# Streaming-encoder trunk in one kernel: raw weight chunks in three slots of their own, another plan of parked and summed pairs

## The chip, the cores and the metric

One core of a Trainium2 chip runs the whole program in one launch. The metric is the device time of one execution in microseconds, the median over the runs. Profiled executions are read beside it; their span is the time from the first to the last instruction that the profiler saw.

## What is computed

Two layers over 256 positions of width 2048, all in float32. Layer 0 mixes tokens with a gated MLP with a spatial gate (gMLP), layer 1 with latent attention (MLA); both are followed by a gated MLP with a causal convolution of width 3, and each sublayer is added to its input and normalised:

```
def reference(x, ...):
    for i in range(DEPTH):                      # DEPTH = 2
        if i % N_MIXERS == 0: m = gmlp_mixer(x, ...)   # gelu(x @ w_in), layer_norm(v), gate, @ w_out
        else:                 m = mla_mixer(x, ...)    # low-rank q and kv, rotary keys, softmax, @ w_out
        x = layer_norm(ALPHA * x + m, ln_mix_g[i], ln_mix_b[i])
        f = conv_ffn(x, ...)                    # x @ w_up, convolution, silu(g) * a, @ w_down
        x = layer_norm(ALPHA * x + f, ln_ffn_g[i], ln_ffn_b[i])
    return x
```

The weights are w_in 2048 x 12288, gMLP's w_out 6144 x 2048, the MLA matrices, and for each layer w_up 2048 x 11008 and w_down 5504 x 2048.

## The kernel before

**Precision.** TensorE multiplies a reduced form of float32 (fp32r). Each float32 operand is split into a high part (a cast on ScalarE) and a low part (operand minus high part, a subtraction on VectorE), and a product takes three matmuls: high x high, low x high, high x low. All weights pass through this once: a chunk of 1 MB (128 x 2048 float32) is loaded as `raw`, ScalarE writes `wh`, VectorE writes `wl`.

**Stages.** In order: v (half of the gMLP input product, six groups of 1024 columns), u (the other half), wo (gMLP output), up0 and dn0 (the MLP of layer 0), the MLA part (mq, mkv, qr, qn, kn, vv, attention, mo), up1 and dn1. Each has a list of weight chunks; the lists are one sequence of 444 chunks, numbered from 0.

**Feed.** The class `Feed` runs through this sequence. `_load` issues a chunk's transfer on SyncE's queue (line 92 or 97), `_split` issues its cast and subtraction (lines 119, 120), and `next` keeps about two chunks split and two more loaded ahead of the chunk in use. `behind` ties each load to the last matmul issued before it in the program, so that the scheduler doesn't pull it far ahead. All these tiles (raw, wh, wl, and the activations) take slots of one pool, tag `big`, 17 slots of 8 KB per partition; a new tile takes the slot that was free first and waits for its last reader.

**Seven products.** In v, wo and dn the rows of the weight come in pairs of chunks of 128. A pair of two 128-row blocks by two 512-column blocks needs eight block products; a Winograd-like form needs seven, if four sums of the weight blocks (and of the activations) are made first. Such a pair is "seven" (`_seven`, lines 127 to 134: tile `ts` for the sums, cast and subtraction of `wh`, `wl`, `th`, `tl`), the others are "wide". Seven products spare 3 matmuls of 128 x 512 in each pair and cost VectorE and ScalarE the sums and their split. The seven sums are put together in the end by `rest` and added to the residual by `fold` (lines 431 to 434, 634).

**Parked.** For dn some pairs with seven products are split long before, during the up projection, where VectorE has time (`park`): the four results (tiles pwh, pwl, pth, ptl) are written to DRAM (`kept...`) and fetched back on GpSimd's queue (`_fetch`, line 185, tiles fwh, fwl, fth, ftl). These tiles have tag `side`, six slots.

**The plan.** `PLAN` lists for each half of the output columns the order of the pairs and the kind of each: `8s` is pair 8 with seven products, `8p` the same and parked, `8e` wide. A down projection has 22 units per half; before, 18 of 44 have seven products, 8 of these parked. `KEEP` says how many chunks ahead the activations of a kind (dn...wx, sx, px) are kept from the first half for the second.

**The end of a down projection.** The last three chunks (`SKEW`) are kept, and their products go to the accumulators one after the other, q3, p2, e and q4, so that LayerNorm (`piece`, `start`, `scale`, lines 640 to 659) can begin on the first while TensorE still works on the last. In dn1 the result then goes out to DRAM (line 659).

**What sets the order.** The program's instructions are put in order for each engine by a list scheduler, which works from the dependencies, the slots and a cost model; only what is wrapped in `keep_in_program_order` stays where it is written. So a change of slots moves instructions in many places. Within an engine the order is then fixed: an instruction that waits holds up all behind it. SyncE's order of transfers is fixed in the same way.

Of the kernel before, what the change touches and what calls it, by code (L numbers as in the profile page):

```python
# [15 lines left out]
P = 128  # L16
# [35 lines left out]
T1, T2 = 6, 5  # L52
SLOTS = {"big": 17, "side": 6}

# [17 lines left out]
class Feed:  # L72
# [73 lines left out]
    def park(self, i):  # L146
# [3 lines left out]
        add = lambda o, a, b: pin(nc.vector.tensor_tensor(o, a, b, ALU.add))  # L150
        two = lambda a, o: a[:, o : o + 1024].rearrange("p (n c) -> p n c", n=2)
        self.kept[i] = kept = {}
# [11 lines left out]
        yield  # L164
        t = tile("pts", F32)
        add(two(t, 0), two(raw, 512), raw[:, None, 0:512].to_broadcast([P, 2, 512]))
        add(t[:, 1024:1536], t[:, 0:512], raw[:, 1024:1536])
        add(t[:, 1536:2048], t[:, 1024:1536], raw[:, 1536:2048])
        yield
        for n, src, o, cols in (("w", raw, 512, 1536), ("t", t, 0, 2048)):  # L170
            hi, lo = tile(f"p{n}h", F32R), tile(f"p{n}l", F32R)
            pin(nc.scalar.copy(hi[:, 0:cols], src[:, o : o + cols]))
            pin(nc.vector.tensor_tensor(lo[:, 0:cols], src[:, o : o + cols], hi[:, 0:cols].bitcast(F32), ALU.subtract))
# [5 lines left out]
    def _fetch(self, i):  # L179

        got = []
        for n in ("wh", "wl", "th", "tl"):
            d = self.kept[i].pop(n)
            t = self.pool.tile([P, 2048], F32R, tag="side", name=f"f{n}{i}", bufs=SLOTS["side"])
            self.behind(self.nc.gpsimd.dma_start(t[:, 0 : d.shape[1]], d))
            got.append(t)
        return got

# [8 lines left out]
    def next(self, splits=2, loads=2):  # L197
        i = self.used
        self.ahead(i + 1 + splits + loads, i + 1 + splits)
        self.used += 1  # L200
        return self.parts.pop(i)


@with_exitstack
def trunk(ctx: ExitStack, tc: tile.TileContext, x, xT, gm_in, gm_wout, ffn_up, ffn_dn,
# [86 lines left out]
    for j in range(4):  # L292
        t = slot([P, 4, S], f"xraw{j}")

# [102 lines left out]
    class Banks:  # L397
# [16 lines left out]

        def seven(self, a, sums, wh, wl, th, tl):
            s1, s2, s3, s4 = sums
# [55 lines left out]
    def down(n_k, src, tag, ln, acts, skew=SKEW):  # L472
# [5 lines left out]
        for hf, units in enumerate(seq):  # L478
# [3 lines left out]
            for i, (u, kind) in enumerate(units):  # L482
# [13 lines left out]
                else:  # L496
                    acc.seven(a, sums, *got)
                    if u == last:
# [196 lines left out]
    for gi in range(6):  # L695
# [3 lines left out]
        for c, p in enumerate(V_PAIRS[gi]):  # L699
# [12 lines left out]
            if c == 2 and gi > 0:  # L712
                stats(gi - 1)
        vt = slot([P, 2, 1024], f"v{gi}", tag="side")
        for i, (n, t) in enumerate(zip(DIRECT, rest)):
# [6 lines left out]
        if gi == 0:  # L722
# [4 lines left out]
            nc.sync.dma_start(lnrow, ln_rows.rearrange("r (k p) -> (r k) p", p=P))  # L727
        if gi == 4:

            wT = slot([P, 2, 1024], "wT")  # L730
            wTg = wT[:, 0, :].rearrange("p (g i) -> p g i", g=NG)
            nc.sync.dma_start(wTg, w_sT)
            nc.gpsimd.memset(wTg[64:P, :, 0:64], 0.0)
            bsum = slot([P, 2, 1024], "bsum")
            nc.sync.dma_start(bsum[:, 1, :], b_s.to_broadcast([P, 1024]))
    stats(5)
    lnt = bank("lnrowT")
    nc.tensor.transpose(lnt[:, 0:P], lnrow, ident)
    nc.scalar.copy(lncol, lnt[:, 0:P])
    ones = tp.tile([P, P], F32, tag="t1", name="ones", bufs=T1)  # L740
    nc.gpsimd.memset(ones, 1.0)
    for f in range(2):
        rb = bank(f"rows{f}")
        mm(rb, ones, wT[:, 0, f * 512 : (f + 1) * 512], True, True)
        nc.scalar.copy(bsum[:, 0, f * 512 : (f + 1) * 512], rb)
    mv = [st.tile([P, 4], F32, tag="vmv", name=f"vmv{b}", bufs=2) for b in range(2)]
# [14 lines left out]
    rowsum = bsum[:, 0, :].rearrange("p (g i) -> p g i", g=NG)  # L761
    bsb = bsum[:, 1, :].rearrange("p (g i) -> p g i", g=NG)

# [489 lines left out]
```

## Time and profile before

| | us |
|---|---|
| median of the runs shown | 2502.89 |
| all three runs | 2502.18, 2502.89, 2507.27 |
| the profiled execution's own time | 2503.74 |
| its span | 2501.9 |
| TensorE, VectorE, ScalarE busy | 2472.1, 1987.7, 1425.2 |

The profiled execution is one more run of the same kernel; 1.84 us of its time lie outside of its span. Where a stage's length is given, it runs from one boundary that a view was asked for to the next. In the rows of a timeline the first number is the start, the second how long it took, and in brackets stands how long the engine was idle before and for what it waited. In the rows of windows, the window's bounds are followed by its length, then by each engine's busy time with its number of instructions (TensorE's matmuls, its weight loads, VectorE, ScalarE, GpSimd), the granted clock, the DMA engines' busy share, and GB/s.

### The profile page before, as it was taken

Reading aid. Unit: us, or ns where it says so; the run is one execution under the profiler, and the core shown is the slowest. Engines: PE = TensorE matmul, PEld = TensorE weight load, DVE = VectorE, ACT = ScalarE, POOL = GpSimd, SP = SyncE. Lnnn points to the kernel's source line nnn. Section 1 sums busy time; section 2 is a strip of 40 time slices with the busy share of each in tenths; the row PEclk is TensorE's granted clock in tenths of the full one; section 3 lists DMA queues with packets and bytes.
Section 4 is the critical chain, followed back from the end, with each engine's and each line's share of the span. In section 5 each row is a group of like instructions: output and inputs, shape, how many; then the busy total and the mean of one; then the engine's idle time right before and its main releaser. Section 6 shows DMA issues by size and latency. Waiting matters only on the chain.

```text
span 2501.9 us, 33396 instructions
## 1 busy us (share of the span) xinstructions
PE 2472.1 (99%) x12995; PEld 2123.2 (85%) x12995; DVE 1987.7 (79%) x2779; ACT 1425.2 (57%) x1976; POOL 84.8 (3%) x165
## 2 busy tenths in 40 slices
PE   9999999999999999999999999999999999999998
PEld 7887888888888888888887878988888888887886
DVE  6999866679898798796678878856698787768887
ACT  5666644456565666565555456564566665555543
POOL 0000000000000010000000100000000000000010
PEclk9999999999999999999999999999999999999999
DMA  6555644556566689787547984543589789556795
GB/s 245 201 217 203 218 170 169 185 178 216 201 201 214 247 337 356 293 331 277 185 168 286 341 323 165 181 168 129 189 315 352 277 340 361 200 173 231 278 375 196
DMA packets 109503, 606.17 MB, mean 242 GB/s; under 512 B 10272, under 2 KB 11040, under 8 KB 62112
## 3 DMA queue, kind: packets, MB, share of 16 engines
q1 hardware_dynamic: 85984, 465.61, 52.0%
q0 software_dynamic: 23360, 138.42, 14.1%
q8 instruction: 102, 1.67, 0.2%
q14 instruction: 57, 0.47, 0.1%
HBM read 538.98 MB, written 65.01 MB: 241 GB/s over the span
## 4 chain that ended last, share of the span: by engine, by line
PE 87%; DVE 5%; DMA 4%; issue 2%; ACT 1%; SPq 0%; POOL 0%; DVEq 0%; ACTq 0%; POOLq 0%
PE up L225 35%; PE u L225 11%; PE wo_q L225 5%; PE v_q L225 4%; PE dn_q L225 4%; PE mo L225 4%; PE v_p L225 4%; PE wo_p L225 3%; PE dn_p L225 3%; DMA raw<-in_ffn_dn_dram 3%; PE wo_e L225 2%; PE upf L225 2%; PE v_e L225 1%; DVE wl L120 1%; PE dn_e L225 1%
## 5 line engine op out<-in xcount | busy, mean ns | idle before, releaser
L120 DVE TENSOR_TENSOR wl<-raw,wh 128x1024 fp32r<-128x1024 f32 (+3 forms) x640 | 877.9, 1392 | 241.4 <-ACT wh L119 211.4
L119 ACT CAST wh<-raw 128x1024 fp32r<-128x1024 f32 (+3 forms) x640 | 743.4, 1189 | 336.2 <-DVE wl L120 71.2
L225 PE MATMUL up<-xhl,wh 128*128 128x512 f32 x2624 | 611.1, 390 | 0.0
L225 PEld LDWEIGHTS up<-xhl,wh 128*128 128x128 f32 x2624 | 487.4, 188 | 97.7
L225 PEld LDWEIGHTS up<-xhl,wl 128*128 128x128 f32 x2624 | 325.8, 192 | 6.4
L225 PE MATMUL up<-xhl,wl 128*128 128x256 f32 x2624 | 328.1, 283 | 0.0
L225 PE MATMUL u<-xhl,wh 128*128 128x512 f32 x768 | 182.5, 392 | 0.2 <-DVE h_u L380 0.2
L225 PEld LDWEIGHTS u<-xhl,wh 128*128 128x128 f32 x768 | 141.7, 188 | 29.0 <-DVE h_u L380 0.7
L127 ACT CAST th<-ts 128x1536 fp32r<-128x1536 f32 x106 | 111.2, 1052 | 86.4 <-DVE ts L134 76.0
L128 DVE TENSOR_TENSOR tl<-ts,th 128x1536 fp32r<-128x1536 f32 x106 | 126.4, 1219 | 0.6 <-ACT th L127 0.2
L225 PEld LDWEIGHTS u<-xhl,wl 128*128 128x128 f32 x768 | 95.6, 191 | 3.1 <-DVE wl L120 1.0
L127 ACT CAST wh<-raw 128x1536 fp32r<-128x1536 f32 x53 | 78.5, 1481 | 33.6 <-DVE wl L120 8.3
L225 PE MATMUL u<-xhl,wl 128*128 128x256 f32 x768 | 96.6, 283 | 0.8 <-DVE wl L120 0.8
L128 DVE TENSOR_TENSOR wl<-raw,wh 128x1536 fp32r<-128x1536 f32 x53 | 92.9, 1752 | 0.5 <-PE wo_p L225 0.4
L225 PE MATMUL mo<-wh,oT 128*128 128x512 f32 x256 | 82.6, 403 | 0.0
L134 DVE TENSOR_TENSOR ts<-raw 128x1024 f32<-128x1024 f32 x53 | 64.7, 1220 | 17.4 <-DMA raw<-in_ffn_dn_dram 10.4
L225 PE MATMUL v_q<-wh,xhl 128*128 128x512 f32 x224 | 70.2, 395 | 4.6 <-ACT wh L119 4.6
L134 DVE TENSOR_TENSOR ts<-ts,raw 128x512 f32<-128x512 f32 x106 | 72.7, 686 | 0.8
L225 PE MATMUL v_p<-wh,xhl 128*128 128x512 f32 x192 | 61.0, 395 | 1.0 <-ACT wh L119 1.0
L225 PEld LDWEIGHTS v_q<-wh,xhl 128*128 128x128 f32 x224 | 42.4, 190 | 14.4 <-ACT wh L119 5.7
L378 ACT COPY lo_u<-u 128x256 f32<-128x256 f32 x48 | 17.4, 362 | 60.0 <-PE u L225 60.0
L225 PEld LDWEIGHTS mo<-wh,oT 128*128 128x128 f32 x256 | 45.4, 189 | 7.1
(1703 smaller groups left out, 4255.2 us busy)
## 6 DMA issues: line engine op xcount, KB each, us to landing
raw<-in_ffn_up_dram SPq DMA_DIRECT2D x172, 1024.0 KB, 6.6
raw<-in_gm_in_dram SPq DMA_DIRECT2D x93, 1024.0 KB, 4.7
raw<-in_ffn_dn_dram SPq DMA_DIRECT2D x68, 1024.0 KB, 7.9
raw<-in_gm_wout_dram SPq DMA_DIRECT2D x48, 1024.0 KB, 5.1
praw<-in_ffn_dn_dram POOLq DMA_DIRECT2D x16, 1024.0 KB, 15.3
keptth<-pth POOLq DMA_DIRECT2D x16, 1024.0 KB, 9.4
kepttl<-ptl POOLq DMA_DIRECT2D x16, 1024.0 KB, 11.6
fth<-keptth POOLq DMA_DIRECT2D x16, 1024.0 KB, 9.2
```

The costliest lines, as they stand in the source:

```text
L119: self.nc.scalar.copy(hi[:, c], raw[:, c])
L120: self.nc.vector.tensor_tensor(lo[:, c], raw[:, c], hi[:, c].bitcast(F32), ALU.subtract)
L127: self.nc.scalar.copy(hi, raw)
L128: self.nc.vector.tensor_tensor(lo, raw, hi.bitcast(F32), ALU.subtract)
L134: add = lambda o, a, b: self.nc.vector.tensor_tensor(o, a, b, ALU.add)
L225: recent[0] = nc.tensor.matmul(o, l, r, start=start, stop=stop, skip_group_check=True)
L378: nc.scalar.copy(lo, acc[:, S : 2 * S])
```

## The change

**Slots.** The pool's 17 shared slots become 14, and three slots of a tag `raw` are added, which take the raw chunks only. The four pieces of the input `xraw` move from `big` to `side`. Two of the gMLP tables (`bsum` and `wT`) share fewer slots and are loaded a group later.

**Plan.** The plan of the down projection changes: parked pairs at 1, 6, 11, 15 in the first half and 19, 15, 11, 7 in the second, and nine with seven products that are not parked; 17 in all instead of 18.

**Fetch.** A parked pair is fetched when it lies within five chunks of the one in use (`LEAD`), and not when the loader comes to it.

**Park.** The sums of a parked pair are made in place, in the raw tile, by four adds of 512 columns, after the raw blocks themselves were split; the sums lie in another order, so `seven` has an offset `turned`.

**Pace.** `behind` ties no load to a matmul until the first chunk is in use.

```diff
-SLOTS = {"big": 17, "side": 6}
+SLOTS = {"big": 14, "raw": 3, "side": 6}
...
-        NF_FF: ("0e 1e 2s 3e 4p 5s 6e 7e 8s 9e 10e 11p 12s 13e 14e 15s 16e 17s 18p 19e 20e 21e",
-                "21e 20p 19e 18p 17s 16e 15p 14s 13e 12e 11p 10s 9e 8e 7p 6s 5e 4e 3e 2e 1e 0e")}
+        NF_FF: ("0e 1p 2e 3s 4e 5e 6p 7e 8s 9e 10e 11p 12e 13s 14e 15p 16e 17s 18e 19s 20e 21e",
+                "21e 20e 19p 18e 17s 16e 15p 14e 13s 12e 11p 10e 9s 8e 7p 6e 5s 4e 3e 2e 1e 0e")}
...
-KEEP = {"wide": 5, "seven": 9, "parked": 6}
+LEAD = 5
+KEEP = {"wide": 4, "seven": 6, "parked": 6}
...
         if kind == "parked":
-            self.parts[self.loaded] = self._fetch(self.loaded)
+            self.fetch(self.loaded)
             self.loaded += 1
             return
-        t = self.pool.tile([P, 2048], F32, tag="big", name=f"raw{self.loaded}", bufs=SLOTS["big"])
+        t = self.pool.tile([P, 2048], F32, tag="raw", name=f"raw{self.loaded}", bufs=SLOTS["raw"])
...
-        t = tile("pts", F32)
-        add(two(t, 0), two(raw, 512), raw[:, None, 0:512].to_broadcast([P, 2, 512]))
-        add(t[:, 1024:1536], t[:, 0:512], raw[:, 1024:1536])
-        add(t[:, 1536:2048], t[:, 1024:1536], raw[:, 1536:2048])
-        yield
-        for n, src, o, cols in (("w", raw, 512, 1536), ("t", t, 0, 2048)):
+        for n, o, cols in (("w", 512, 1536), ("t", 0, 2048)):
...
             if n == "w":
                 yield
+                r = [raw[:, 512 * i : 512 * (i + 1)] for i in range(4)]
+                add(r[1], r[1], r[0])
+                add(r[0], r[0], r[2])
+                add(r[2], r[2], r[1])
+                add(r[3], r[3], r[2])
+                yield
...
-        return self.parts.pop(i)
+        got = self.parts.pop(i)
+        near = [j for j in range(i + 1, min(i + 1 + LEAD, len(self.chunks))) if self.chunks[j][2] == "parked"]
+        if near and near[0] in self.kept:
+            self.fetch(near[0])
+        return got
...
-        if recent[0] is not None:
+        if recent[0] is not None and feed.used > 0:
...
-        t = slot([P, 4, S], f"xraw{j}")
+        t = slot([P, 4, S], f"xraw{j}", tag="side")
...
-            self.to("q5", s1, th, tl, 0)
-            self.to("p7", s3, th, tl, 512)
+            self.to("q5", s1, th, tl, turned)
+            self.to("p7", s3, th, tl, 512 - turned)
...
-                    acc.seven(a, sums, *got)
+                    acc.seven(a, sums, *got, 512 if kind == "parked" else 0)
```

Three places show how the order of instructions moves. The first is SyncE at the program's start, where the input `xraw`, the tables `cst` and `rope_sb` and the first weights are loaded. Before:

```order
1 L296 DMA xraw_90<-in_xT_dram 128x256 x4
2 L723 DMA cst<-in_consts_dram 128x792
3 L724 DMA rope_sb<-in_ropes_dram 128x128
4 L97 DMA raw_92<-in_gm_in_dram 128x512 x4
5 L727 DMA lnrow<-in_ln_rows_dram 128x128
6 L97 DMA raw_118<-in_gm_in_dram 128x1024 x2
```

And now:

```order
1 L302 DMA xraw_90<-in_xT_dram 128x256
2 L98 DMA raw_92<-in_gm_in_dram 128x512 x2
3 L302 DMA xraw_90<-in_xT_dram 128x256
4 L98 DMA raw_92<-in_gm_in_dram 128x512 x2
5 L302 DMA xraw_90<-in_xT_dram 128x256 x2
6 L98 DMA raw_118<-in_gm_in_dram 128x1024 x2
```

The first weight pieces stand between the pieces of the input, and the tables are gone from here: they come behind the tenth chunk.

The second is VectorE between dn0 and the MLA products: `xhl` are the normalised activations (lny) split, `hqk` is a normalised latent, and the `wl` of 128 x 864 are the key/value weights (mkv). Before:

```order
1509 L676 TENSOR_TENSOR xhl_1_12819<-lny_1_1_12984,xhl_1_12819 128x4x128
1510 L343 RECIPROCAL rms_12997<-rms00q 128x1
1511 L918 TENSOR_SCALAR hqk<-mq_12869,rms_12997 128x512
1512 L120 TENSOR_TENSOR wl_13025<-raw_12927,wh_13024 128x864 x2
1513 L676 TENSOR_TENSOR xhl_2_12820<-lny_1_2_13017,xhl_2_12820 128x4x128
1514 L120 TENSOR_TENSOR wl_13057<-raw_13030,wh_13056 128x864
1515 L676 TENSOR_TENSOR xhl_3_12821<-lny_1_3_13049,xhl_3_12821 128x4x128
```

And now:

```order
1495 L682 TENSOR_TENSOR xhl_1_12818<-lny_1_1_12983,xhl_1_12818 128x4x128
1496 L349 RECIPROCAL rms_12996<-rms00q 128x1
1497 L923 TENSOR_SCALAR hqk<-mq_12868,rms_12996 128x512
1498 L121 TENSOR_TENSOR wl_13024<-raw_12926,wh_13023 128x864
1499 L682 TENSOR_TENSOR xhl_2_12819<-lny_1_2_13016,xhl_2_12819 128x4x128
1500 L121 TENSOR_TENSOR wl_13024<-raw_12926,wh_13023 128x864
1501 L682 TENSOR_TENSOR xhl_3_12820<-lny_1_3_13048,xhl_3_12820 128x4x128
```

The order of the first rows is the same, but `wl_13024` now takes a slot whose last reader is a later matmul, and `xhl_2` stands between its two halves.

The third is TensorE near the program's end. `dn_q_20920` and `dn_q_20899` are the accumulator q3 of the second half, `dn_q_20923` and `dn_q_20902` are q4, and `wh_21587` and `wh_21571` belong to the last chunk. Before, q3 gets its last product here:

```order
10846 L225 MATMUL dn_q_20920<-wh_21587,dn11wx 128x512
10847 L225 MATMUL dn_q_20920<-wl_21588,dn11wx 128x512
10848 L225 MATMUL dn_q_20920<-wh_21587,dn11wx 128x512 x2
10849 L225 MATMUL dn_q_20920<-wl_21588,dn11wx 128x512
10850 L225 MATMUL dn_p_20921<-wh_21587,dn11wx 128x512
```

And now here:

```order
10868 L231 MATMUL dn_q_20899<-wh_21571,dn10wx 128x512 x2
10869 L231 MATMUL dn_q_20899<-wl_21572,dn10wx 128x512
10870 L231 MATMUL dn_p_20900<-wh_21571,dn10wx 128x512
10871 L231 MATMUL dn_p_20900<-wl_21572,dn10wx 128x512
10872 L231 MATMUL dn_p_20900<-wh_21571,dn10wx 128x512 x2
10873 L231 MATMUL dn_p_20900<-wl_21572,dn10wx 128x512
10874 L231 MATMUL dn_e<-wh_21571,dn10wx 128x512
10875 L231 MATMUL dn_e<-wl_21572,dn10wx 128x512
10876 L231 MATMUL dn_e<-wh_21571,dn10wx 128x512 x2
10877 L231 MATMUL dn_e<-wl_21572,dn10wx 128x512
```

Behind the last of these rows come two matmuls of q4 with the chunk before and six with the last chunk, then the program ends; before, 49 matmuls stand behind row 10849, of which the last 24 are q4's.

More of the change, by code (lines that the diff above doesn't have):

```diff
@@ L150, in park @@
         add = lambda o, a, b: pin(nc.vector.tensor_tensor(o, a, b, ALU.add))
-        two = lambda a, o: a[:, o : o + 1024].rearrange("p (n c) -> p n c", n=2)
         self.kept[i] = kept = {}
@@ L164, in park @@
         yield
-        t = tile("pts", F32)
-        add(two(t, 0), two(raw, 512), raw[:, None, 0:512].to_broadcast([P, 2, 512]))
-        add(t[:, 1024:1536], t[:, 0:512], raw[:, 1024:1536])
-        add(t[:, 1536:2048], t[:, 1024:1536], raw[:, 1536:2048])
-        yield
-        for n, src, o, cols in (("w", raw, 512, 1536), ("t", t, 0, 2048)):
+        for n, o, cols in (("w", 512, 1536), ("t", 0, 2048)):
             hi, lo = tile(f"p{n}h", F32R), tile(f"p{n}l", F32R)
-            pin(nc.scalar.copy(hi[:, 0:cols], src[:, o : o + cols]))
-            pin(nc.vector.tensor_tensor(lo[:, 0:cols], src[:, o : o + cols], hi[:, 0:cols].bitcast(F32), ALU.subtract))
+            pin(nc.scalar.copy(hi[:, 0:cols], raw[:, o : o + cols]))
+            pin(nc.vector.tensor_tensor(lo[:, 0:cols], raw[:, o : o + cols], hi[:, 0:cols].bitcast(F32), ALU.subtract))
             store(f"{n}h", hi, cols)
@@ L177, in park, with fetch @@
                 yield
-    def _fetch(self, i):
-        got = []
+                r = [raw[:, 512 * i : 512 * (i + 1)] for i in range(4)]
[4 more added lines that the diff above has]
+                yield
+    def fetch(self, i):
+        if i in self.parts:
+            return
+        got = self.parts[i] = []
         for n in ("wh", "wl", "th", "tl"):
@@ L413, in eight, with seven @@
                         self.to(DIRECT[2 * b + f], a[b][j], hi, lo, j * 1024 + f * 512)
-        def seven(self, a, sums, wh, wl, th, tl):
+        def seven(self, a, sums, wh, wl, th, tl, turned=0):
             s1, s2, s3, s4 = sums
@@ L713, in trunk @@
                 stats(gi - 1)
+            if c == 4 and gi == 5:
+                wT = slot([P, 2, 1024], "wT")
+                wTg = wT[:, 0, :].rearrange("p (g i) -> p g i", g=NG)
+                nc.sync.dma_start(wTg, w_sT)
+                nc.sync.dma_start(wT[:, 1, :], b_s.to_broadcast([P, 1024]))
+                nc.gpsimd.memset(wTg[64:P, :, 0:64], 0.0)
         vt = slot([P, 2, 1024], f"v{gi}", tag="side")
@@ L727, in trunk @@
             nc.sync.dma_start(lnrow, ln_rows.rearrange("r (k p) -> (r k) p", p=P))
[L728 to L735, printed above, removed]
     stats(5)
@@ L739, in trunk @@
     nc.scalar.copy(lncol, lnt[:, 0:P])
+    rsum = slot([P, 1024], "rsum")
     ones = tp.tile([P, P], F32, tag="t1", name="ones", bufs=T1)
@@ L760, in trunk @@
                                     op0=ALU.subtract, op1=ALU.mult)
-    rowsum = bsum[:, 0, :].rearrange("p (g i) -> p g i", g=NG)
-    bsb = bsum[:, 1, :].rearrange("p (g i) -> p g i", g=NG)
+    rowsum = rsum.rearrange("p (g i) -> p g i", g=NG)
+    bsb = wT[:, 1, :].rearrange("p (g i) -> p g i", g=NG)
     pT = [None] * 6
```

3 lines of the change are left out of this document (1 added, 2 removed).

## The prediction

> **What bounds the kernel now.** I read the page's head and slices first, then the busy time by stage, then what the matmuls waited for.
>
> ```profile
> span 2501.9 us, 33396 instructions
> PE 2472.1 (99%) x12995; PEld 2123.2 (85%) x12995; DVE 1987.7 (79%) x2779; ACT 1425.2 (57%) x1976; POOL 84.8 (3%) x165
> PEclk9999999999999999999999999999999999999999
> ```
>
> TensorE is busy for 2472.1 of 2501.9 us at a granted clock that never drops. So there are only 29.8 us that an edit of loads and buffers can win, plus or minus what it does to the number of matmuls. The stages (start to warm-up's end, v, the first down projection, the second one, and the tail) say where these lie:
>
> ```profile
> 0.00:8.45 8.45, 3.82 (x9) 1.20 (x9) 1.68 (x5) 3.50 (x6) 2.00 (x14) 0.99 0.66 195
> 8.45:262.00 253.55, 251.05 (x1092) 206.32 (x1093) 225.30 (x219) 161.88 (x192) 0.52 (x1) 0.99 0.61 222
> 1289.00:1520.00 231.00, 224.23 (x981) 183.12 (x981) 194.77 (x250) 121.66 (x128) 15.09 (x30) 1.00 0.77 282
> 2264.00:2491.00 227.00, 223.34 (x978) 183.07 (x978) 192.83 (x248) 115.05 (x119) 14.87 (x28) 1.00 0.75 281
> 2491.00:2502.00 11.00, 0.03 (x1) 0.00 (x0) 7.10 (x12) 0.29 (x1) 0.00 (x0) 0.60 0.25 96
> ```
>
> The second column is the length, the third TensorE's busy time. TensorE idles 8.45 - 3.82 = 4.63 us before its first real matmul, 2.50 in v, 6.77 in the first down projection, 3.66 in the second and 11 at the end: 28.6 of the 29.8. The view of waits names most of it:
>
> ```profile
> PE v_q L225 <- ACT wh L119: 4.6, 2, 3.3
> PE dn_q L225 <- DVE tl L128: 3.4, 2, 1.7
> PE dn_q L225 <- DVE dn03wx L467: 2.3, 1, 2.3
> PE dn_q L225 <- DMA ftl<-kepttl: 2.1, 2, 1.6
> PE dn_q L225 <- ACT th L127: 1.7, 1, 1.7
> ```
>
> The columns are total, times, longest. 3.3 of the first line is the start, 1.3 lies in v. The next four are the down projections: pair 8 (seven products, raw weights late), the wide activations dn03wx (queued on VectorE behind the fold of the seven-product sums), and the fetch of a parked pair.
>
> A gap costs more than its idle time:
>
> ```profile
> 1481.82 0.62 PE L225 MATMUL dn_q<-th,dn06sx 128*128 128x512 f32 x2
> 1482.50 0.62 PE L225 MATMUL dn_q<-th,dn06sx 128*128 128x512 f32 x2
> 1333.58 0.39 PE L225 MATMUL dn_p<-wl,dn08sx 128*128 128x512 f32 x1
> 1335.66 0.73 PE L225 MATMUL dn_q<-th,dn08sx 128*128 128x512 f32 x2 [1.69 <-ACT th L127]
> ```
>
> Three 128x512 matmuls follow each other in 0.68 us, 0.227 each. Over the gap the distance is 2.08, 1.85 more than 0.227, where 1.69 is shown as idle: 0.16 per gap on top.
>
> **The start.** Before, SyncE issues four pieces of xT and two tables, and only then the first weights:
>
> ```profile
> 0.74 1.81 SPq L296 DMA_DIRECT2D xraw<-in_xT_dram  x4
> 3.55 1.85 SPq L97 DMA_DIRECT2D raw<-in_gm_in_dram  x4
> 7.78 0.62 ACT L119 CAST wh<-raw 128x512 fp32r<-128x512 f32 x1 [2.86 <-DMA raw<-in_gm_in_dram]
> 8.45 1.22 PE L225 MATMUL v_q<-wh,xhl 128*128 128x512 f32 x2 [3.32 <-ACT wh L119]
> ```
>
> One issue takes 1.81/4 = 0.45. In the new order the first weight piece stands behind one xT piece, at 0.74 + 0.45 = 1.2 instead of 3.55: 2.35 us earlier, and everything up to the matmul with it (8.45 to 6.1; the warm-up ends at 5.14, so it is not in the way). The weights then share the DMA engines with the xT pieces behind them, so the gain has a floor of about 1.2 (half lost) and a ceiling of 3.3 (the whole wait). I take **-2.35**.
>
> **Raw chunks in three slots.** Before, pair 8 of the first down projection was late like this (VectorE's rows, then POOL's, then the DMA share, last but one column, of two stretches):
>
> ```profile
> 1325.10 1.23 DVE L134 TENSOR_TENSOR ts<-raw 128x1024 f32<-128x1024 f32 x1 [2.26 <-DMA raw<-in_ffn_dn_dram]
> 1313.64 0.53 POOL L185 DMA_DIRECT2D fwh<-keptwh  x1 [178.10 <-PE dn_p L225]
> 1318.00:1324.00 6.00, 6.00 (x28) 4.99 (x27) 4.64 (x7) 3.06 (x3) 0.00 (x0) 1.00 1.02 343
> 1324.00:1330.00 6.00, 6.00 (x28) 4.95 (x28) 4.90 (x6) 2.97 (x2) 0.00 (x0) 1.00 1.05 409
> 1335.00 0.61 ACT L127 CAST th<-ts 128x512 fp32r<-128x512 f32 x1
> ```
>
> A parked pair's fetch was issued when the raw load was under way, the DMA engines were full, the raw pair landed at 1325.1, and its adds and casts took both engines until 1335.6: 10.5 us. Now pair 8 is a wide chunk, and the summed pairs stand elsewhere. A raw load no longer waits for a matmul to release a slot, but for the split of the raw chunk three before it. In matmul time (0.227 each, counted in both orders) from the last matmul that must be over to the first use, a raw chunk of the first half has 20.3 us in the middle before and 28.9 now, of the second half 20.7 and 27.8. The prices:
>
> ```profile
> raw<-in_ffn_up_dram SPq DMA_DIRECT2D x172, 1024.0 KB, 6.6
> raw<-in_ffn_dn_dram SPq DMA_DIRECT2D x68, 1024.0 KB, 7.9
> ftl<-kepttl POOLq DMA_DIRECT2D x16, 1024.0 KB, 12.7
> L120 DVE TENSOR_TENSOR wl<-raw,wh 128x2048 fp32r<-128x2048 f32 x108 | 246.6, 2288 | 75.8 <-ACT wh L119 72.1 <-issue 3.5
> L119 ACT CAST wh<-raw 128x2048 fp32r<-128x2048 f32 x108 | 206.0, 1911 | 90.2 <-DMA raw<-in_ffn_dn_dram 43.8 <-DMA raw<-in_gm_wout_dram 13.8 <-DMA raw<-in_gm_in_dram 7.2
> ```
>
> Three slots turn once in three chunks of 24 matmuls, 16.3 us. Landing, cast and subtraction of a wide chunk take 7.9 + 1.91 + 2.29 = 12.1, 4.2 less. A summed pair (7.9 + 10.5 = 18.4) takes 2.1 longer and lives on the two to three chunks that are split ahead; there is one in five chunks at most, so it is made good. The two stalls of pair 8 go. The parked pairs stand at least four apart and are fetched five chunks ahead: 18.2 us at least against 8.4, over the 12.7 of the slowest piece, so the ftl waits go. The fold chain now comes a chunk earlier, with two splits between its steps, so the dn03wx wait goes. First down projection: 6.77 idle + 5 gaps x 0.16 = 7.6; second: 3.66 + 4 x 0.16 = 4.3. In v the cast of wh now stands ahead of the gelu and square steps on ScalarE: 1.3 + 0.2 + 0.3 = 1.8. Together **-13.7**. The bounds: from 0, if the DMA engines and not the slots were late, to all of it; I take all, since no chunk's work is longer than its turn for two in a row.
>
> What pays for it are the slots of the split weights, 17 less 3. Seven wide chunks per down projection have 4.8 to 5.7 us from the release of a slot to the first use (5.9 at the least before), against 1.91 + 2.29 = 4.2 for cast and subtraction: 0.6 to 1.5 over, if VectorE is free just then. I take 0, and 1.1 per chunk as the other end (see the slower rival).
>
> The Trainium skill ("Perfetto Trace Analysis", Identifying Performance Opportunities) says that the same gap repeating on the engine that should be saturated can mean that SBUF has too few buffers for the next tile. Today's trace has no such row: its gaps are single ones, with DMA or queue order behind them. If three slots less bring that pattern, it is the slower rival, not the forecast.
>
> **More matmuls, fewer adds.** Ten pairs with seven products become nine per down projection: 3 matmuls of 0.227 each, 0.68, twice: **+1.4**, with TensorE the bound. VectorE loses a few us of adds in 195 busy of 231, which buys nothing by itself. The parked pairs' sums run as four adds of 512 in place, in the up projection, where TensorE has no idle time to lose: 0.
>
> **Boundaries.** The tighter slots show where a stage begins. At the latent key/value products the order puts 1.55 us of matmuls between the release of a slot and the first use of what is split into it:
>
> ```profile
> 1542.06 0.93 ACT L119 CAST wh<-raw 128x864 fp32r<-128x864 f32 x1
> 1543.02 1.06 DVE L120 TENSOR_TENSOR wl<-raw,wh 128x864 fp32r<-128x864 f32 x1 [2.66 <-ACT wh L119]
> ```
>
> Cast and subtraction of a piece take 1.99 to 2.02, so the wait is at least 0.5; with the gap's 0.16, 0.6. At each up projection's start the second weight chunk has 3.6 to 4.3 and stands ahead of the last LayerNorm parts: 0.65 each, between 0 and 1.3. At the value product 3.4 with copies of q and k ahead on ScalarE: 1.3, between 0 and 2. Sum **+3.2** (0.6 to 5.2).
>
> **The tail.** The last chunk's raw slot now comes free with a split that stands behind the fold chain on VectorE, so its matmuls come late, and the last four accumulators end closer together.
>
> ```profile
> 2479.96 0.69 DVE L640 TENSOR_TENSOR res<-res,dn_q 128x512 f32<-128x512 f32 x1 [1.85 <-PE dn_q L225]
> 2488.39 0.68 DVE L640 TENSOR_TENSOR res<-res,dn_e 128x512 f32<-128x512 f32 x1
> 2489.11 0.69 DVE L643 BATCH_NORM_STATS2 lnst<-res 128x6 f32<-128x512 f32 x1
> 2491.07 0.69 DVE L640 TENSOR_TENSOR res<-res,dn_q 128x512 f32<-128x512 f32 x1 [1.26 <-PE dn_q L225]
> 2496.86 1.41 DVE L658 SCALAR_TENSOR_TENSOR res<-res,lnrs,lnb 128x512 f32<-128x512 f32 x2
> 2490.64 0.39 PE L225 MATMUL dn_q<-wl,dn11wx 128*128 128x512 f32 x1
> 2486.51 12.11 SPq L659 DMA_DIRECT2D out_dram<-res  x8
> ```
>
> VectorE needs 2488.39 - 2479.96 = 8.43 us for the first 128 rows, 2489.80 - 2488.39 = 1.41 for e, and 2498.27 - 2491.07 = 7.20 for the last accumulator's part: 17.04 in all. Before, the first accumulator is complete 49 matmuls (11.1 us) before TensorE's end, so only the last part shows: VectorE ends 7.24 us behind it. Now 18 matmuls follow the first accumulator's last one: 4.09 us, 0.04 later VectorE starts, and as all the others (2.95, 1.82, 0 before the end) are complete by the time it gets to them, it ends 17.04 - 4.05 = 12.99 behind TensorE. **+5.7**; the 3.6 us of the output transfer stay. Bounds: 0 if the last chunk were no bottleneck, +6.5 with a wait for its split.
>
> **The sum.** Gains 2.35 + 13.7 = 16.05; costs 1.4 + 3.2 + 5.7 = 10.3: -5.75. The profiled execution took 2503.74 (span 2501.9 and 1.84 around it), so 2498.0; it lies 0.85 over the runs' median of 2502.89, so the median comes to about **2497**. Within 0.2%, which is 5.0 us here, a measurement can't tell a difference: below 2497.9 counts as faster, above 2507.9 as slower.
>
> **Rivals.**
>
> *The end costs less* (13%). If the last chunk's split is through in time, the tail keeps part of its 7.2, and the boundaries hide: the gain is 16.05 - 1.4 - 3 = 11 to 12, 2491. For it: the tail fence above shows VectorE idle for 1.85 and 1.26 us near the end. Against it: the order of the matmuls is fixed, and 18 of them stay 18.
>
> *The stalls move* (12%). Within the down projections the same VectorE queue (195 of 231 us busy) is late for the next chunk, and two thirds of the 11.9 won there come back: 2497 + 8 = 2505, no change. For it: one wait (dn03wx) was queue order, not a load. Against it: the summed pairs are fewer and spread out.
>
> *The loads stay late* (12%): the change doesn't do what it says. If the full DMA engines (share 1.02 and 1.05 above) made pair 8 late and not its slot, the 3.4 + 1.7 and the 2.1 stay: 2497 + 7.2 + 4 x 0.16 = 2505. Against it: the fetch is spread differently now, and a wide chunk needs 4.2 us after landing, not 10.5.
>
> *Too few slots for the split weights* (15%): slower. The fourteen wide chunks with 4.8 to 5.7 us wait whenever VectorE is one subtraction behind as the slot comes free: 4.2 + 2.29 - 5.4 = 1.1 us each and 0.16 for the gap, 17.6 in all; 2497 + 17.6 = 2515. It decides from 0.8 a chunk on (2497 + 11). For it: VectorE is busy 84% of that stage. Against it: v has several chunks with 4.8 to 5.7 now, and waits 1.3 us once and 0.2 once.
>
> **The numbers.** The forecast holds 48%, with 2492 to 2501 as its own range; two thirds of it lie under 2497.9 (32%). With the first rival that makes 0.45 for faster; the other third and the second and third rival 0.40 for no change; the last one 0.15 for slower. The range takes in both ends but the slower rival: 2490 to 2506.
>
> **What would show it.** First real matmul at 6.1 instead of 8.45. No wait for tl or th of a pair and none for ftl in the down projections; TensorE idle there under 2 us each. Short waits at the first mkv and vv products. VectorE's last instruction 13 us after the last matmul instead of 7.2, without any wait on TensorE after the first accumulator. Wrong would be: many waits of about 1 us for wl in the down projections, or a tail of 7 us.

## The result and the profile after

| | before | changed |
|---|---|---|
| median of 7 runs, us | 2505.25 (2502.18 to 2507.27) | 2495.93 (2495.13 to 2498.85) |
| profiled execution, us (span) | 2503.74 (2501.9) | 2497.42 (2495.6) |

The ratio is 0.9967, with a 95% interval of 0.9955 to 0.9978: the changed kernel is 0.33% faster, which is more than the 0.2% that a measurement of it can tell. The forecast was 2497 with 2490 to 2506; as a difference, it was 5.75 us under the three runs that were known then. The two profiled executions stand 6.3 us of span apart, the medians 9.3: the one of before is 1.5 under its median, the changed one 1.5 over it. What follows is worked out from the spans.

The head of the changed kernel's page, then its windows by stage (length, then TensorE's busy time): the start, v, u, dn0, up1 with the boundary ahead of it, dn1 and the tail.

```profile
span 2495.6 us, 33479 instructions
PE 2472.2 (99%) x13001; PEld 2124.7 (85%) x13001; DVE 1983.5 (79%) x2782; ACT 1420.7 (57%) x1973; POOL 84.7 (3%) x165
```

```profile
0.00:5.10 5.10, 3.79 (x10) 1.20 (x10) 0.45 (x2) 2.30 (x3) 2.05 (x14) 1.00 0.53 154
5.10:255.00 249.90, 248.75 (x1094) 205.06 (x1094) 230.80 (x224) 163.22 (x195) 0.52 (x1) 1.00 0.64 231
255.00:551.00 296.00, 293.62 (x1735) 257.92 (x1733) 200.85 (x361) 139.13 (x213) 0.00 (x0) 1.00 0.50 174
1286.80:1509.60 222.80, 222.80 (x986) 184.44 (x985) 187.39 (x244) 116.88 (x124) 15.04 (x30) 1.00 0.82 297
1770.90:2257.30 486.40, 484.03 (x2757) 426.32 (x2756) 380.57 (x544) 293.99 (x434) 25.37 (x45) 1.00 0.74 275
2257.30:2480.00 222.70, 222.70 (x982) 183.82 (x981) 180.11 (x235) 110.77 (x115) 14.79 (x28) 1.00 0.76 284
2480.00:2495.60 15.60, 0.07 (x1) 0.00 (x0) 12.34 (x22) 0.29 (x1) 0.00 (x0) 0.64 0.35 134
```

In both down projections TensorE is now busy from end to end, where it idled 6.77 and 3.66 us before. The tail's row is the other side: 15.60 us instead of 11.00. u and up1 have more idle time than before: 296.00 - 293.62 = 2.4 and 486.40 - 484.03 = 2.4 us, where they had 1.05 and 0.40. The same two stretches before (the two windows are u and up1):

```profile
262.10:554.00 291.90, 290.85 (x1734) 258.40 (x1733) 201.44 (x362) 138.47 (x214) 0.00 (x0) 1.00 0.50 175
1781.30:2264.10 482.80, 482.40 (x2757) 425.05 (x2755) 376.21 (x538) 291.98 (x432) 25.42 (x45) 1.00 0.74 279
```

The waits of the changed kernel's matmuls, the longest groups:

```profile
PE upf L231 <- ACT xhl L681: 1.9, 1, 1.9
PE u L231 <- DVE h_u L386: 1.5, 1, 1.5
PE warm L231 <- POOL idle L273: 1.3, 1, 1.3
PE up L231 <- ACT wh L120: 0.9, 2, 0.5
```

Not one line is of a down projection. For the whole account, this table has the stages' lengths, each from its first matmul to that of the next, for the two kernels and for the experiments. "start" is the first real matmul; "mla" runs from dn0's end to mo's end, "up" from the boundary ahead of it to the down projection, "tail" from the start of the last matmul to the end of the span:

| span, us | start | v + u | wo | up0 | dn0 | mla | up1 | dn1 | tail | sum |
|---|---|---|---|---|---|---|---|---|---|---|
| before | 8.45 | 545.57 | 252.85 | 482.73 | 230.91 | 260.83 | 482.79 | 226.51 | 11.25 | 2501.9 |
| changed | 5.10 | 545.89 | 252.91 | 482.87 | 222.86 | 261.31 | 486.40 | 222.34 | 15.95 | 2495.6 |
| e1 pace | 4.96 | 543.94 | 252.85 | 482.66 | 231.61 | 260.86 | 482.76 | 227.15 | 11.24 | 2498.0 |
| e2 plan | 8.42 | 543.34 | 252.85 | 482.52 | 230.73 | 260.81 | 482.65 | 227.90 | 10.95 | 2500.2 |
| e3 slots | 10.27 | 544.60 | 252.92 | 483.02 | 226.95 | 261.27 | 486.44 | 224.59 | 16.68 | 2506.7 |
| e4 shared | 4.77 | 542.66 | 252.87 | 482.61 | 227.76 | 260.82 | 482.61 | 226.47 | 10.84 | 2491.4 |
| e5 last raw | 4.78 | 545.88 | 252.91 | 482.91 | 222.86 | 261.23 | 486.43 | 222.36 | 15.95 | 2495.3 |
| e6 rows, pin | 4.97 | 543.74 | 252.91 | 484.81 | 222.86 | 261.37 | 486.49 | 222.16 | 10.84 | 2490.1 |
| e7 15 + 2 | 4.78 | 551.90 | 258.50 | 516.39 | 240.87 | 262.22 | 517.20 | 239.96 | 10.88 | 2602.7 |
| e8 no lead | 5.08 | 546.11 | 252.91 | 483.38 | 222.85 | 261.24 | 484.92 | 222.35 | 15.95 | 2494.8 |
| e9 rows, mo | 5.34 | 546.04 | 252.93 | 482.89 | 222.86 | 261.42 | 482.84 | 222.16 | 10.86 | 2487.3 |
| e10 e9 + pin | 4.64 | 544.17 | 252.91 | 483.31 | 222.86 | 261.29 | 482.82 | 222.16 | 10.84 | 2485.0 |

So the change won 3.35 at the start, 8.05 in dn0 and 4.17 in dn1 (which hold 1.36 us more matmuls), and lost 4.70 in the tail, 3.61 at up1 and some tenths elsewhere. v and u stand in one column because e4 mixes them; apart, the changed kernel won 3.78 in v (253.65 to 249.87) and lost 4.10 in u (291.92 to 296.02). How far one execution differs from another can be read where two kernels have the same instructions in the same order. That holds for changed, e5, e8 and e9 from the start to mo: their u is 296.0 to 296.9, their v 249.2 to 249.9. It holds for before and e2 up to the end of u: their v is 253.65 and 251.42. So one or two us in a single stage of a single profile can be chance, where a stage has waits (dn0, which has none left, is 222.86 in all four).

### The profile page after: what moved, and what is told of

Read it like the earlier page. It is cut to its first block, busy times and chain, and to the rows that moved or that the text cites. A ratio compares the mean times of both kernels' runs of the same rounds, so it can differ in the third digit from the quotient of the medians.

```text
span 2495.6 us, 33479 instructions
## 1 busy us (share of the span) xinstructions
PE 2472.2 (99%) x13001; PEld 2124.7 (85%) x13001; DVE 1983.5 (79%) x2782; ACT 1420.7 (57%) x1973; POOL 84.7 (3%) x165
## 5 line engine op out<-in xcount | busy, mean ns | idle before, releaser
L231 PEld LDWEIGHTS u<-xhl,wh 128*128 128x128 f32 x768 | 141.0, 188 | 33.3 <-issue 3.8
L128 ACT CAST th<-ts 128x1536 fp32r<-128x1536 f32 x102 | 105.7, 1052 | 83.4 <-DVE ts L135 52.4
L129 DVE TENSOR_TENSOR tl<-ts,th 128x1536 fp32r<-128x1536 f32 x102 | 120.6, 1217 | 8.7 <-PE dn_p L231 3.4
L231 PE MATMUL mo<-wl,oT 128*128 128x512 f32 x128 | 50.2, 392 | 0.0
```

What stands on the lines that cost most here:

```text
L128: self.nc.scalar.copy(hi, raw)
L129: self.nc.vector.tensor_tensor(lo, raw, hi.bitcast(F32), ALU.subtract)
L231: recent[0] = nc.tensor.matmul(o, l, r, start=start, stop=stop, skip_group_check=True)
```

## The experiments

**e1: the pace alone.** One line of the change in the kernel before:

```diff
-        if recent[0] is not None:
+        if recent[0] is not None and feed.used > 0:
```

> The kernel before with one line of the change: no load is tied to a matmul until the first chunk is in use. The order of SyncE's first transfers becomes the changed kernel's, all else stays. Theory (the start is a term of its own): first real matmul at 5.1 us instead of 8.45, all later stages as before, profiled span 2501.9 - 3.4 = about 2498.5, v's own idle time shorter by up to 1.5 because the second piece of weights is early too. Rival (the early start only moves the wait, since v is fed by loads in a row): v's stage becomes longer by what the start wins, span 2501 or more.

2499.96 us, ratio 0.9988 (0.9978 to 0.9998), span 2498.0. The start is 3.49 earlier and v is 1.63 shorter (253.65 to 252.02), the later stages stay within 0.7. The theory holds, and the start is a term by itself that needs none of the rest. Part of it was not a wait. Before, the matmuls behind the start ran at half clock (granted clock third from the end, before and then the changed kernel):

```profile
8.45:14.00 5.55, 4.56 (x10) 3.16 (x11) 2.85 (x5) 2.92 (x5) 0.00 (x0) 0.50 1.01 354
```

```profile
5.10:14.00 8.90, 7.75 (x30) 5.57 (x30) 6.10 (x10) 6.02 (x10) 0.00 (x0) 1.00 0.98 368
```

10 matmuls in 5.55 us at 0.50 against 30 in 8.90 at 1.00: the wait of 3.32 us behind the warm-up had taken the warm-up's clock away again (1.00 from 4.80 to 8.21, with TensorE busy for 0.34 us of that, and 0.50 from there on).

**e2: the plan alone.** The kernel before with the two lines of `PLAN` changed, nothing else.

> The kernel before with the changed plan alone: 17 shared slots, old fetch, old start. Theory (raw slots clear the waits of summed pairs, the plan only those of the fetch): the two ftl waits (0.5 and 1.6 us) go, 1.4 us of matmuls are added, other waits for raw weights of 3 to 5 us stay in the two down projections at whichever summed pairs come behind a fetch; span 2500 to 2502; tail 11 us as before. Rival (the plan alone spreads the work): the down projections have no wait over 0.6 us left, span 2501.9 - 13.6 + 1.4 = 2490.

2502.98 us, ratio 0.9991 (0.9981 to 1.0), span 2500.2: no change beyond what can be told. Its waits in the down projections:

```profile
PE dn_q L225 <- DVE wl L128: 2.9, 2, 2.0
PE dn_q L225 <- DVE wl L120: 2.5, 2, 1.3
...
PE dn_q L225 <- DVE dn00wx L467: 1.2, 1, 1.2
PE dn_q L225 <- DVE dn02wx L467: 1.1, 1, 1.1
PE dn_q L225 <- DVE tl L128: 1.1, 2, 0.5
```

The ftl waits are gone, as the theory said, and so are those of pair 8; others of about the same sum stand in their place. dn0 is 0.18 shorter than before and dn1 1.39 longer, with 0.68 of added matmuls in each. With shared slots the plan only moves the stalls.

**e3: the slots alone.** The old plan, fetch and pace:

```diff
-SLOTS = {"big": 17, "side": 6}
+SLOTS = {"big": 14, "raw": 3, "side": 6}
...
-        t = self.pool.tile([P, 2048], F32, tag="big", name=f"raw{self.loaded}", bufs=SLOTS["big"])
+        t = self.pool.tile([P, 2048], F32, tag="raw", name=f"raw{self.loaded}", bufs=SLOTS["raw"])
...
-        t = slot([P, 4, S], f"xraw{j}")
+        t = slot([P, 4, S], f"xraw{j}", tag="side")
```

> The kernel before with the slots alone: 14 shared, 3 for raw chunks, the input pieces in the side slots; old plan, old fetch. Its start is later (seven input pieces ahead of the first weights): first matmul at 9 to 11. Theory: pair 8's waits (3.4 and 1.7 us) go, the ftl waits stay (2.1), the tail is 4.7 longer, u 4 longer; span 2501.9 - 6 + 4.7 + 4 + 1 = 2505. Rival (the raw slots do nothing for the down projections, the plan does): pair 8's waits stay, span 2510.

2510.56 us, ratio 1.0022 (1.0012 to 1.0031), span 2506.7, the theory's 2505. Of its waits:

```profile
PE v_q L225 <- ACT wh L119: 4.9, 1, 4.9
PE dn_q L225 <- DMA ftl<-kepttl: 4.3, 2, 2.3
PE upf L225 <- ACT xhl L675: 1.9, 1, 1.9
...
PE dn_q L225 <- ACT th L127: 0.8, 1, 0.8
```

The last row is what is left of pair 8's waits: 0.8 us in all, where it was 3.4 + 1.7. The fetch still waits (and for longer: the next thing that was late). The 3.96 and 1.92 us won in dn0 and dn1 are less than what the slots cost: 5.4 in the tail, 3.65 at up1, 2.8 in u.

**e4: the changed kernel with 17 shared slots.** The first two edits of e3 undone, all else as changed.

> The changed kernel, but with 17 shared slots as before, raw chunks among them; plan, fetch, start and parking as changed. Theory (three raw slots cost the tail, u and the last boundary, and win in the down projections): tail back at 11 us instead of 16, u back at 292 instead of 296, the up1 boundary without its 2 us wait: -12; the down projections take back some of their 13.6, the waits of summed pairs for raw weights: +4 to +8; span 2487 to 2491. Rival (all gains of the down projections came from the plan and the fetch, none from the slots): no wait over 0.6 us in the down projections, span 2495.6 - 12 = 2483.

2493.73 us, ratio 0.9959 (0.9944 to 0.9974), span 2491.4. Tail, up1 and mla are back at their lengths of before; dn0 and dn1 are 4.9 and 4.1 longer than in the changed kernel, 9.0 in all, just above the theory's 4 to 8. The waits there are of the kind that e2 shows:

```profile
PE dn_q L231 <- DVE wl L129: 2.6, 2, 1.8
...
PE dn_q L231 <- DVE dn00wx L473: 1.2, 1, 1.2
PE dn_q L231 <- DVE tl L129: 1.1, 2, 0.5
PE dn_q L231 <- DVE dn12wx L473: 1.0, 1, 1.0
```

Together with e2 and e3 this takes plan and slots apart. In dn0 + dn1: 457.4 before, 458.6 with the plan, 451.5 with the slots, 454.2 with plan, fetch and parking but shared slots, 445.2 with all. So the slots won 5.9 by themselves and 9.0 on top of the rest; the rest won 3.2 without the slots and 6.3 with them, the plan by itself nothing. What in the rest wins (parking in place, the shorter `KEEP`, the order that follows) was not taken apart. By the spans the slots' own balance in the changed kernel is a loss of 4.2 (2491.4 against 2495.6); the two ratios' intervals overlap.

**e5: the last raw chunk in a side slot.**

```diff
+        tag = "side" if self.loaded == len(self.chunks) - 1 else "raw"
-        t = self.pool.tile([P, 2048], F32, tag="raw", name=f"raw{self.loaded}", bufs=SLOTS["raw"])
+        t = self.pool.tile([P, 2048], F32, tag=tag, name=f"raw{self.loaded}", bufs=SLOTS[tag])
```

> The changed kernel with one raw chunk, the program's last, in a side slot instead of a raw slot, so that its load waits for no split any more. Theory of the prediction (the last chunk is late because its raw slot comes free late): VectorE's split of the last chunk starts some 5 us earlier against the last matmul, the accumulators end apart again, tail 11 us, span 2491. Rival (the late part is the shared slot of wl, three fewer of which remain, and the LayerNorm rows lng and lnb take two of these 14): nothing changes, tail 16 us, span 2495 to 2496.

2497.07 us in a single run, span 2495.3, tail 15.95 as in the changed kernel. The rival holds. Three rows of it: SyncE loads the last chunk, ScalarE casts it, and VectorE makes `wl` 23 us after the load was issued.

```profile
2448.49 0.38 SPq L94 DMA_DIRECT2D raw<-in_ffn_dn_dram  x1
```

```profile
2460.20 1.92 ACT L121 CAST wh<-raw 128x2048 fp32r<-128x2048 f32 x1 [3.52 <-DMA raw<-in_ffn_dn_dram]
```

```profile
2471.27 2.29 DVE L122 TENSOR_TENSOR wl<-raw,wh 128x2048 fp32r<-128x2048 f32 x1 [6.68 <-issue]
```

In the changed kernel the same load was issued at 2458.14, so the raw slot did come free late there; but `wl` began at 2471.58, hardly later than here. The raw data and `wh` were there 9 us before `wl` began, and VectorE stood idle for 6.68 of them. The profile doesn't name what it waited for; e6 and e9 show it to be a shared slot.

**e6: the rows of the last LayerNorm in side slots, u's casts pinned.**

```diff
-            self.g = slot([P, D], f"lng{i}")
+            self.g = slot([P, D], f"lng{i}", tag="side")
...
-            self.b = slot([P, D], f"lnb{i}")
+            self.b = slot([P, D], f"lnb{i}", tag="side")
...
-            self.nc.scalar.copy(hi[:, c], raw[:, c])
+            cast = self.nc.scalar.copy(hi[:, c], raw[:, c])
+            if 48 <= i < 96:
+                self.pin(cast)
```

> The changed kernel with two edits. The rows lng and lnb of the last LayerNorm lie in side slots instead of shared ones; and in u the casts of wh are pinned behind what stands before them in the program on ScalarE, so none stands ahead of a copy of u that releases an accumulator. Theory (14 shared slots cost the tail through wl's slot and u through the cast's place): tail 11 us instead of 16, u 292 to 293 instead of 296, all else as in the changed kernel: span 2495.6 - 4.7 - 3.6 = 2487. Rival (the tail comes from the raw slot, u from the moved load of wT): span 2495.

2491.22 us, ratio 0.9937 (0.9924 to 0.9949), span 2490.1. The tail is 10.84: `lng` and `lnb` had held two of the 14 shared slots just when the last chunk needed them. u came down by 1.6 (294.39), not by the 3.6 expected, and up0 was 1.9 longer. The reason for the pin, in the changed kernel's u (ScalarE, then VectorE, then TensorE):

```profile
306.63 1.04 ACT L120 CAST wh<-raw 128x1024 fp32r<-128x1024 f32 x1 [0.25 <-PE u L231]
...
307.90 0.35 ACT L384 COPY lo_u<-u 128x256 f32<-128x256 f32 x1
```

```profile
308.28 0.42 DVE L386 TENSOR_TENSOR h_u<-u,lo_u 128x256 f32<-128x256 f32 x1 [0.60 <-ACT lo_u L384]
```

A cast that itself waited for a slot (0.25, released by a matmul of u) stands ahead of the copy `lo_u`, VectorE's `h_u` waits 0.60 for that, and the next matmul into this accumulator waits for `h_u`: it starts 0.41 behind the one before it instead of 0.23. This comes back nine times in u, every 24.3 us, 1.6 us in all, and with the pin it is gone.

**e7: 15 shared slots and 2 for raw chunks**, with `lng` and `lnb` in side slots.

```diff
-SLOTS = {"big": 14, "raw": 3, "side": 6}
+SLOTS = {"big": 15, "raw": 2, "side": 6}
```

> The changed kernel with 15 shared slots and 2 raw ones, lng and lnb in side slots. Theory (a raw slot turns once in as many chunks as there are slots, 5.45 us each: two give 10.9 us against 12.1 for landing, cast and subtraction): waits for raw weights come back in the down projections, 5 to 15 us in all, while tail and last boundary win 8: span 2492 to 2503. Rival (loads are issued ahead far enough, the number of raw slots does not matter, shared slots do): no such waits, span 2484 to 2488.

2608.47 us, ratio 1.041 (1.0393 to 1.0427): 4.1% slower, and 107 us of span over the changed kernel, where the theory gave 5 to 15 us of waits. Its direction was right, but it had looked at the down projections alone. They lose 18 each; the two up projections lose 33.5 and 31 (against the changed kernel), because the casts there wait for their loads again and again. Of the 33.5, 19.2 are idle time of TensorE and 14.4 slower matmuls: the granted clock is 0.97 over that stage. What ScalarE waited for here, what TensorE waited for here, and what ScalarE waited for in the changed kernel:

```profile
ACT wh L120 <- DMA raw<-in_ffn_up_dram: 275.8, 103, 9.3
ACT wh L120 <- DMA raw<-in_ffn_dn_dram: 104.3, 31, 9.2
```

```profile
PE up L231 <- ACT wh L120: 26.7, 10, 3.5
...
PE up L231 <- DVE wl L121: 6.6, 10, 1.8
```

```profile
ACT wh L120 <- PE u L231: 85.5, 37, 3.6
ACT wh L120 <- PE up L231: 72.5, 41, 4.1
ACT wh L120 <- DMA raw<-in_ffn_up_dram: 65.2, 24, 5.4
```

With three raw slots the casts wait mostly for a shared slot, with two for their data. This is a pattern that the Trainium skill ("Perfetto Trace Analysis", Identifying Performance Opportunities) has as a possible sign of too few buffers: the same gap over and over on the engine that should be saturated. The trace agrees: ScalarE waits 103 times for a load in the up projections, and TensorE, which should be saturated, idles 20 times there for a chunk's split, 33.3 us in all. In the changed kernel TensorE waits twice for a cast there, 0.9 us, and shows no such pattern, as the forecast had it.

**e8: no lead for the fetch** (`LEAD = 1`).

> The changed kernel without the new fetch rule: a parked pair is fetched when the loader comes to it, as before. Theory (the fetch waits for the four side slots of the parked pair before it, so the spacing of the plan sets when it starts, not the rule): no ftl wait, same stages within 0.5 us, span 2495 to 2496. Rival (the five chunks' lead made the fetch early): ftl waits of 0.5 to 2 us come back in both down projections, span 2497 to 2499.

2496.55 us in a single run, span 2494.8, no ftl wait. The fetch rule does nothing: the loader still fetches a parked pair when it comes to it, and with `LEAD = 1` every engine runs the changed kernel's instructions in the changed kernel's order. The plan's spacing is what clears the ftl waits, since they are gone in e2 too, with the old fetch; that it works through the side slots of the parked pair before is likely, and not shown.

So e8 is the changed kernel once more, and its up1 is 1.48 shorter. The wait at up1's start is the same in both, 1.9 us, but here the clock didn't fall behind it (last section). Of the 3.61 that the changed kernel lost at up1, 1.5 hang on that.

**e9: `lng` and `lnb` in side slots, and one chunk fewer split ahead at the end of mo.**

```diff
-        hi, lo = feed.next(splits=2 if left > 5 else 3 if left > 2 else 4, loads=2 if left > 2 else 1)
+        hi, lo = feed.next(splits=2 if left > 5 else 3, loads=2 if left > 2 else 1)
```

> The changed kernel with lng and lnb in side slots and, in the last loop of the attention's output product, at most three chunks split ahead instead of four, so that one chunk's casts fewer stand ahead of the LayerNorm parts on ScalarE at the start of up1. Theory (the 2 us wait at up1's start is those casts, and the matmuls at half clock behind it follow from the wait): boundary 20 us instead of 23.5, tail 10.5 instead of 16, all else as in the changed kernel, u 296 and up0 456: span 2495.6 - 5.4 - 3.5 = 2486.7. Rival (the wait moves to the next LayerNorm part, or the chunk split later is late for up1): boundary 22 or more, or a wait for wh at up1; span 2489 to 2491.

2489.12 us, ratio 0.9935 (0.9921 to 0.9949), span 2487.3 as the theory said. up1 is back at 482.84. What had happened there, on ScalarE before, then in the changed kernel, then in e9:

```profile
1778.56 2.00 ACT L119 CAST wh<-raw 128x1024 fp32r<-128x1024 f32 x2
```

```profile
1768.28 3.89 ACT L120 CAST wh<-raw 128x1024 fp32r<-128x1024 f32 x4
```

```profile
1768.82 2.00 ACT L120 CAST wh<-raw 128x1024 fp32r<-128x1024 f32 x2
```

Four casts instead of two stood ahead of the last of `lny`, and the first matmul of up1 waited 1.9 us. The clock made it more, in the changed kernel's windows from that wait on:

```profile
1771.50:1773.40 1.90, 0.04 (x1) 0.00 (x0) 1.90 (x3) 1.90 (x5) 0.00 (x0) 1.00 0.41 65
1773.40:1775.20 1.80, 1.76 (x10) 1.69 (x11) 1.79 (x3) 1.80 (x5) 0.00 (x0) 0.78 0.87 355
1775.20:1777.50 2.30, 2.30 (x7) 1.71 (x7) 1.63 (x4) 2.30 (x7) 0.00 (x0) 0.50 1.04 431
```

Busy all the time in the last of them, but at 0.50: 7 matmuls in 2.30 us.

**e10: e9 with u's casts pinned as in e6.**

> The kernel of the run before this one, with u's casts of wh pinned as well. Theory (the pin wins 1.6 us in u, and the 2.0 us that up0 lost in the earlier run with the pin came with it, through the slots that follow from the other order): u 294.4, up0 457.7, the same time within 1 us. Rival (the loss in up0 had another cause): up0 455.7, span 2485.

2487.19 us, ratio 0.9925 (0.9911 to 0.9939), span 2485.0. u is 294.13, as in e6, and up0 483.31 where e6 had 484.81: the rival is nearer. Up to mo, e6 and e10 run the same instructions in the same order, so the 1.5 between their up0 is one execution's difference from another and not an edit's doing. This is the fastest of the kernels: by the medians 18.8 us under the kernel before in the same runs (2506.02).

## Why the prediction was right, and where it was not

The terms of the sum against the profiled spans:

| term | predicted | measured |
|---|---|---|
| start | -2.35 | -3.35 |
| v | -1.8 | -3.78 |
| down projections, their waits | -11.9 | -13.6 (-12.22, with 1.36 of added matmuls in it) |
| added matmuls | +1.4 | +1.36 |
| boundaries | +3.2 | +4.2 (up1 3.6, mla 0.5, up0 0.1) |
| u | 0 | +4.1 |
| tail | +5.7 | +4.7 |
| sum | -5.75 | -6.3 |

**The down projections went as predicted**, and e3 and e4 show that the slots did the larger part of it (5.9 to 9.0 of the 12.2). Pair 8's waits, the ftl waits and the dn03wx wait are all gone, and no other came: the tight slots of the split weights, the ground of the slower rival, cost nothing there. One detail of the step was wrong. The five chunks' lead has no part in it (e8).

**The start and v were mis-sized, each for its own reason.** The first weights went out 2.37 earlier (issued at 1.18 instead of 3.55), as forecast. But they also took 0.98 less from issue to cast (4.43 - 1.18 = 3.25, before 7.78 - 3.55 = 4.23), where the forecast's floor had them take longer; that is the missing 1.0 of the start. In v, "at a granted clock that never drops" was read off slices of 62 us; the window from 8.45 to 14.00 has 0.50, and the forecast had no term for the slow matmuls. The wait for the cast of `wh`, which it did name, is gone. How much of the 3.78 the clock is worth can't be told: in e2 v runs in the order of before, and it was 2.23 shorter there, with 0.50 for 3.4 us (8.61 to 12.03) instead of 6.8. Against e2 the changed v won 1.5.

**The boundaries' sum was near, their places were not.** mkv and vv, 1.9 us of the forecast, have no row among the waits. The two up boundaries were forecast alike; up0 lost 0.14 and up1 3.61, for four casts ahead of `lny` (2.1, by e8) and the clock that fell in the wait (1.5, by e8 a matter of chance). The forecast went over VectorE's and ScalarE's order for the chunks with tight slots, and did not ask which cast comes too early once a raw chunk is there sooner.

**u was left out.** It was put at nothing without a sentence, and cost 4.1. e6 and e10 show about 2 of it as casts ahead of accumulator copies (294.1 and 294.4 against 296.0 to 296.9 in the four executions without the pin); the other half stays open (a wait for `h_u` near 282 us grew from 0.4 to 1.6 lost and is in it).

**The tail was right in mechanism and size, and wrong in its cause.** 18 matmuls stayed behind the first accumulator, VectorE ended 12.3 us behind TensorE (12.99 forecast, its steps overlap a little more), and the output transfer was 0.4 shorter:

```profile
2476.03 0.69 DVE L646 TENSOR_TENSOR res<-res,dn_q 128x512 f32<-128x512 f32 x1 [1.55 <-PE dn_q L231]
...
2491.00 1.41 DVE L664 SCALAR_TENSOR_TENSOR res<-res,lnrs,lnb 128x512 f32<-128x512 f32 x2
```

But "the last chunk's raw slot now comes free with a split" was not what held it: with that slot out of the way the load was issued 9.65 us earlier and the tail stayed at 15.95 (e5), with two shared slots more the tail was back (e6, e9).

Misses of both signs, +1.0 in the tail, -1.0 at the start, -2.0 in v, +4.1 in u, nearly cancel. The forecast of the whole was better than that of its parts, and that was luck.

## What to carry to other kernels

A buffer of its own for the data that arrives, sized to its turn (landing plus what empties it, against the time of one chunk), takes the load off the release order of everything else; here three slots were enough and two cost 4%. It is the pool that gave the slots that pays for this: look at the places where it is fullest, the last loads of a program and the boundaries between stages, and at tiles that lie there without need. Moving two such tiles and one early split won 8.3 us of span (1.5 of it the clock's at up1), more than the 6.3 of the change itself.

## What the runs showed of the hardware

The granted clock fell to 0.50 behind short waits, and stayed there for 3.4 or 6.8 us. The Trainium skill ("TensorE: Matmul & The Clock Gate", Part 1) has the clock halved after an idle window of about 3.4 us that runs freely. The runs bear out the free running: in each trace all changes of the granted clock lie a whole number of 3.413 us apart, the 32 of e7 too. And they show that the window need not be idle throughout: in e7 the nine waits of 2.0 to 3.6 us in the up projections (time lost, start to start) were all followed by 5 to 12 matmuls at 427 ns instead of 227, and at up1 of the changed kernel one of 1.9 us was. The window that held this wait, and the next (TensorE's busy time is the third column, the clock the third from the end):

```profile
1770.98:1774.39 3.41, 1.51 (x12) 1.20 (x11) 3.41 (x4) 3.41 (x8) 0.00 (x0) 1.00 0.46 125
1774.39:1777.81 3.42, 3.42 (x11) 2.80 (x10) 2.75 (x6) 3.42 (x10) 0.00 (x0) 0.50 1.02 424
```

It is not the wait's length alone that decides. In e8, with the same instructions and the same wait of 1.9 us, a bound lies in the middle of the wait and gives each window a part of it. The clock stayed:

```profile
1769.74:1773.15 3.41, 2.43 (x13) 1.81 (x11) 3.15 (x3) 3.41 (x6) 0.00 (x0) 1.00 0.01 2
1773.15:1776.57 3.42, 2.50 (x15) 2.11 (x15) 3.39 (x6) 3.42 (x10) 0.00 (x0) 1.00 0.90 321
```

In the kernel before, a wait of 2.3 us cost nothing more: in the window from 1496.42 to 1499.83 TensorE was busy for 1.73 us of 3.41. Counted over all twelve traces, 22 windows ended with a fall of the clock, and TensorE was busy in them for 10% to 55% of the time; of the 8,680 that ended without one, a single one was busy for less than 48% (43%). So in these runs the clock fell when TensorE had been idle for more than about half of a window. The shares are estimates, as the ends of matmuls are modelled.

e7's longest wait, at 943.5 to 947.3 us:

```profile
943.50:947.30 3.80, 0.33 (x3) 0.06 (x1) 2.50 (x7) 2.33 (x5) 0.02 (x1) 0.81 1.00 420
947.30:952.00 4.70, 4.70 (x11) 3.73 (x12) 4.70 (x7) 3.97 (x6) 0.00 (x0) 0.50 0.97 325
```

11 matmuls in 4.70 us: the wait cost twice, once as idle time and once as clock.
